# Compressed keys and values of the paged cache: two sequences per matmul, half of the head dimension per gathered buffer

## The chip, the cores and the metric

The kernel runs on one core of one Trainium2 chip. The metric is the device time of one execution in microseconds, as the median of several runs. Names used below: TensorE (PE; its weight loads are PEld), VectorE (DVE), ScalarE (ACT), GpSimd (POOL) and SyncE (SP, which only issues transfers).

## What is computed

One inference step of a decoder layer, for a prompt group (1 sequence of 512 tokens) and a sample group (8 sequences of 4 new tokens, each with 2048 past tokens in a paged cache). Three token mixers run in parallel (causal pooling, sparse attention, a diagonal state space), each gated, merged and projected. The part that matters here is the compressed branch of the sparse attention: blocks of 64 past tokens are each folded into one key and one value per head.

```
past = cache_kv[l][page_table].reshape(bd, past_len, N_KV_ROWS, N_KV_HEADS, HEAD_DIM)
blk = full.reshape(b, nb, BLOCK, N_KV_ROWS, N_KV_HEADS, HEAD_DIM)
kc = jnp.einsum('bnlkd,lde->bnke', blk[:, :, :, 0] + pe_cmp[0][:, None, :], w_phi[0])
vc = jnp.einsum('bnlkd,lde->bnke', blk[:, :, :, 1] + pe_cmp[1][:, None, :], w_phi[1])
```

There are 8 sequences, 16 pages of 128 tokens each, 4 key/value heads of dimension 64, blocks of 64 tokens, so two blocks to a page and 32 to a sequence. The sum over a block's 64 tokens and 64 channels is a contraction of length 4096 per head.

## The kernel before, in words

A dense stream of weight tiles runs through the whole kernel, in an order written out by hand. One unit is a weight block of 128 × 1024; `step` (line 167) issues, in this order: the transfers put off by the step before (`run_deferred`), one slice of each background generator in `bg`, the evacuations due, `w_split` and `w_load` (lines 126 to 146) for later units, and the unit's dense matmuls (`mm3`, lines 148 to 151, three for each product, because float32 is split into a high and a low part). A weight load is issued by SP and waits there until one of three raw buffers is free; a unit's weights are loaded three units ahead and split by ScalarE and VectorE two units ahead. Each engine, and SP's and POOL's queues too, works its instructions off in the order in which the program issues them.

The background generator `main_bg` (line 1623) begins at the seventh step (u = 6) with `g_compress` (line 604), which handles the cache; the state space, the compressed prompt keys, the attention of the prompt and of the samples follow in the same generator.

`g_compress` loads the compression weights `wphi` and works through 16 jobs: 8 sequences times keys and values (k = 0, 1). A job's tile `ca` is 128 partitions × 16 pages × 256 floats, and there are two such tiles, so that one job is fetched while another is used. The partition holds one of two head halves and the token's place in its block; the 256 floats of a page are 4 (two blocks of the page by two heads, `m`), 2 (`k`, called kv2 in the loop) and 32 (`e`, the channels of one half of the head dimension).

`fetch` (line 614) gathers pages. `gather` (line 583) sends pages with an odd index through SP, which reads the page number into a register (lines 585 and 586) and issues a plain transfer, and pages with an even index through GpSimd as an indirect transfer (line 589) that takes its 128 row numbers from IDX. The tiles of jobs 0 and 1 are free at the start; the gathers of a later job wait until the matmuls of the job two before have left the buffer. The first four steps fetch the first job, four pages each. Then each job takes three steps: in a step, 6, 5 and 5 pages of the next job are issued, then the matmuls of 11, 11 and 10 channels `d`.

For each channel `d` there are two matmuls (kv2 = 0, 1; line 632), each with a weight of 128 × 64 in one half of the array's columns and 64 moving columns, one for each page and `m`, which lie 64 floats apart in the tile:

```
t = tiles[n].rearrange("q g (m k e) -> q (g m) k e", m=4, k=2)
pe.matmul(acc_b[kv2 * 64:(kv2 + 1) * 64, :64], lhsT=wphi[:, k, d, :],
          rhs=t[:, :, kv2, d], start=(d == 0), stop=(d == 31))
```

They accumulate over d = 0 to 31 in the PSUM bank `s` (two buffers). ScalarE copies 128 × 64 into `KC` at the end of a job (line 635). A float32 matmul shows as two records in the profile, so line 632 has 16 × 32 × 2 × 2 = 2048. The same GpSimd gathers fetch keys and values (`gk`, `gv`) for the attention of the samples later. Line 875 (state space, 72 moving columns) and line 1244 (attention of the prompt, 128 moving columns) are float32 matmuls with the same 128 × 64 weight shape, whose moving columns lie next to each other.

Of the kernel before, what the change touches and what calls it, by code (L numbers as in the profile page):

```python
# [10 lines left out]
F32 = mybir.dt.float32  # L11
F32R = mybir.dt.float32r
I32 = mybir.dt.int32
AF = mybir.ActivationFunctionType
# [52 lines left out]
def kernel(ctx, tc, a):  # L67
    nc = tc.nc
    pe, dve, act, pool, sp = nc.tensor, nc.vector, nc.scalar, nc.gpsimd, nc.sync
    ctx.enter_context(tc.manual_schedule())  # L70

    def P(name, bufs=1, **kw):
        return tc.tile_pool(name=name, bufs=bufs, **kw)

    def R(name, bufs=1):
        return tc.tile_pool(name=name, bufs=bufs, side="right")
# [9 lines left out]
    def bank(tag, bufs):  # L86
        return psb.tile([128, 512], F32, name=tag, tag=tag, bufs=bufs)
# [28 lines left out]
    ones = consts.tile([128, 128], F32, name="ones")  # L116
    epsb = consts.tile([128, 1], F32, name="epsb")

    # ---------------------------------------------------------------- dense stream
    raw, whi, wlo = {}, {}, {}  # L120
    lo_eng = [dve]
    early = [False]
# [36 lines left out]
    state = {"u": 0}  # L159
# [37 lines left out]
            fn()  # L197
            mid.pop(0)

    # ---------------------------------------------------------------- start: x, first weights  # L200
    xr_s = ExitStack()
    xr_p = xr_s.enter_context(P("xr"))
    XH, XL, XR = [], [], []
    first = wraw_p.tile([128, 8, 128], F32, name="wr")
# [98 lines left out]
            after.append(lambda hf=hf: rms_spread(hf))  # L303
        xr_s.close()

    # ---------------------------------------------------------------- pools of the first part
    att_s = ExitStack()
    kc_p = att_s.enter_context(P("kc", side="right"))
    KC = kc_p.tile([128, 2, 8, 64], F32, name="kc")
# [3 lines left out]
    KN = kc_p.tile([128, 2, 2, 32], F32, name="kn")  # L313
    GQ = kc_p.tile([128, 4, 48], F32, name="gq")

    # ---------------------------------------------------------------- evacuation of in-projection tiles
    done = set()
    sub = {}

# [256 lines left out]
                later(lambda t=t, i=2 * gi + md: sp.dma_start(ypool[i], t))  # L576
        step(u, mms, evac)

    # ---------------------------------------------------------------- compressed keys and values
    IDX = consts.tile([128, 128], I32, name="idx")  # L580
    PT = consts.tile([1, 128], I32, name="ptrow")

    def gather(dst, table, col):
        if col % 2:
            r = sp.value_load(PT[0:1, col:col + 1], min_val=0, max_val=NPOOL - 1)
            sp.dma_start(dst, a[table].rearrange("(g p) x -> g p x", p=128)[bass.ds(r, 1)]
                         .rearrange("g p x -> (g p) x"))
        else:
            pool.indirect_dma_start(out=dst, out_offset=None, in_=a[table],  # L589
                                    in_offset=bass.IndirectOffsetOnAxis(ap=IDX[:, col:col + 1], axis=0))  # L590

    def make_idx():
        pi = consts.tile([128, 1], I32, name="pidx")
        pool.iota(pi, pattern=[[0, 1]], base=0, channel_multiplier=1)
        pf = consts.tile([128, 1], F32, name="pidxf")
        dve.tensor_copy(pf, pi)
        sp.dma_start(PT, a["pt"])
        sp.dma_start(IDX, a["pt"].to_broadcast([128, 128]))
        f = consts.tile([128, 128], F32, name="idxf", bufs=1)
        dve.tensor_copy(f, IDX)  # L600
        dve.tensor_scalar(f, f, 128.0, pf, op0=OP.mult, op1=OP.add)
        dve.tensor_copy(IDX, f)

    def g_compress():
        with ExitStack() as s:
            cp = s.enter_context(R("cmp"))
            wphi = cp.tile([128, 2, 32, 64], F32, name="wphi")
            sp.dma_start(wphi, a["wphi"])
            ca_s = ExitStack()
            cap = ca_s.enter_context(R("ca", 2))  # L610
            jobs = [(b, k) for b in range(8) for k in range(2)]
            tiles = {}

            def fetch(n, pages):
                if n >= len(jobs):
                    return
                b, k = jobs[n]
                if n not in tiles:
                    tiles[n] = cap.tile([128, 16, 256], F32, name="ca")
                for pg in pages:  # L620
                    gather(tiles[n][:, pg, :], f"c{k}", b * 16 + pg)
            for pg in range(0, 16, 4):
                fetch(0, range(pg, pg + 4))
                yield
            for n, (b, k) in enumerate(jobs):
                t = tiles[n].rearrange("q g (m k e) -> q (g m) k e", m=4, k=2)
                acc_b = bank("s", 2)
                for d0, d1, pgs in ((0, 11, (0, 6)), (11, 22, (6, 11)), (22, 32, (11, 16))):
                    fetch(n + 1, range(*pgs))
                    for d in range(d0, d1):  # L630
                        for kv2 in range(2):
                            pe.matmul(acc_b[kv2 * 64:(kv2 + 1) * 64, :64], lhsT=wphi[:, k, d, :],  # L632
                                      rhs=t[:, :, kv2, d], start=(d == 0), stop=(d == 31))
                    yield
                act.activation(KC[:, k, b, :], acc_b[:, :64], AF.Copy)
            yield
            ca_s.close()
        done.add("cache")
# [35 lines left out]
                dve.tensor_scalar(KCP[:, k, :16], KCP[:, k, :16], KCP[:, k, 16:17], None, op0=OP.add)  # L674
                dve.tensor_scalar(KC[:, k], KC[:, k], KCP[:, k, 16:17], None, op0=OP.add)

    # ---------------------------------------------------------------- state space
    SSM = {}
    par_s = ExitStack()

# [343 lines left out]
        par_s.close()  # L1024
        done.add("ssm")

    # ---------------------------------------------------------------- attention of the prompt
    def g_prompt():
        while not all(("q", i) in done for i in range(8)):
            yield  # L1030
# [251 lines left out]
        s.close()  # L1282
        done.add("prompt")

    # ---------------------------------------------------------------- attention of the samples
    def g_decode():
        s = ExitStack()
        dp = s.enter_context(R("dec", 2))
# [253 lines left out]
        s.close()  # L1542
        done.add("decode")

    # ---------------------------------------------------------------- operands of the branches
    YH, YL = {}, {}
    yps = {}

# [59 lines left out]
                yz[k] = (y, z)  # L1608
            yield

    # ---------------------------------------------------------------- run the first part
    make_idx()

    def g_copy():
# [8 lines left out]
    def main_bg():  # L1623
        yield from g_compress()
        early[0] = True
        yield from g_ssm()
        early[0] = False
        yield from g_compress_prompt()
        yield from g_prompt()
        yield from g_decode()  # L1630
        early[0] = True
        att_s.close()
        open_y()
        yield from prep_y(0, ypool, "pz")
        yield from prep_z()
# [38 lines left out]
            fn()  # L1674
    xs.close()

    # ---------------------------------------------------------------- branches
    acc_p = ctx.enter_context(P("accp", 17))
    lg_p = ctx.enter_context(P("lgp", 3))
    xo_p = ctx.enter_context(P("xo", 24))  # L1680
# [134 lines left out]
    for u in range(first_tail, len(UNITS)):  # L1815
# [9 lines left out]
        else:  # L1825
# [4 lines left out]
            m, half = un[1:] if un[1] < 14 else ((14, 0), (15, 0), (14, 1), (15, 1))[u - len(UNITS) + 4]  # L1830
# [7 lines left out]
    normalize(1, range(16))  # L1838


# ------------------------------------------------------------------------------ host side
def col_lists():
    off = np.cumsum([0, 1024, 1024, 1024, 1536, 48, 1024, 1024, 1024, 6144])
    pu, pz, q, kv, ag, az, su, sz, mg = off[:9]
    hd = []
    for p in range(2):
        for g in range(4):
            hd.append(np.concatenate([((2 * p + k) * 4 + g) * 64 + np.arange(64) for k in range(2)]))
    ssm = []
    for i in range(8):  # L1850
        c, g = np.meshgrid(np.arange(2 * i, 2 * i + 2), np.arange(64), indexing="ij")
        ssm.append((g * 16 + c).reshape(-1))
    agc = []
    for j in range(3):
        for p in range(2):
            for g in range(4):
                for k in range(2):
                    agc.append(((2 * p + k) * 4 + g) * 3 + j)
    r = np.arange(128)
    return dict(hd=hd, ssm=ssm, cols={  # L1860
        "pu": [pu + 128 * i + r for i in range(8)], "pz": [pz + 128 * i + r for i in range(8)],
        "q": [q + h for h in hd], "az": [az + h for h in hd],
        "kv": [kv + 128 * i + r for i in range(12)],
        "ag": [ag + np.array(agc + [agc[0]] * 80)],
        "su": [su + s for s in ssm], "sz": [sz + s for s in ssm],
        "mg": [mg + 128 * i + r for i in range(48)]})
# [138 lines left out]
```

## Time and profile before

| | |
|---|---|
| time, median of 3 runs | 2476.44 us (2473.95 to 2479.65) |
| profiled execution, first to last instruction | 2475.4 us |
| TensorE busy | 2345.3 us, 95% |
| VectorE, ScalarE, GpSimd busy | 1111.0, 652.3, 419.9 us |
| line 632 (compression of the cache), matmul busy | 141.5 us in 2048 records, from 84.2 to 573.6 us of the span |
| GpSimd's gathers into `ca` | 128, 126.8 us |
| moved by DMA | 358.32 MB, mean 145 GB/s |

How to read it: the profile is of one execution, and only its span is shown, without what lies around it; the span is 1.0 us under the median. Times of records on TensorE overlap, as matmuls are pipelined: the pace of a burst is its length less one record, over the number of records less one. Some records are missing from the trace, so counts in a stretch are a few per cent low. [...]

### The profile page before, as it was taken

To read this page: it belongs to the slowest core of one execution; us is meant where nothing else is said; L and a number is where in the kernel's file an instruction comes from. 1 tells how busy PE (TensorE), PEld (TensorE's weight loads), DVE (VectorE), ACT (ScalarE), POOL (GpSimd) and SP (SyncE) were. 2 spreads that over 40 slices of the span, in tenths; PEclk is the share of its full clock that TensorE was granted. 3 is DMA by queue.
4 is the path that set the end of the run, shared out by engine and by line. 5 is a ranking of instruction groups with operands and counts; after the bars stand their busy time and mean duration, and the time that the engine had idled before them with its cause. 6 is when DMAs were issued, how large, how long until landed. Compare 5 with 4: busy or idle time off the path is not lost.

```text
span 2475.4 us, 49565 instructions
## 1 busy us (share of the span) xinstructions
PE 2345.3 (95%) x20454; PEld 2236.5 (90%) x20454; DVE 1111.0 (45%) x2157; ACT 652.3 (26%) x1117; POOL 419.9 (17%) x387
## 2 busy tenths in 40 slices
PE   8888888999978999999999999889999999999995
PEld 7888888899978999999999898779999999999995
DVE  6223334114498324676666333322452545554225
ACT  5101111112311111444544222222342222222331
POOL 3122222213235200000000214551000001200003
PEclk9898989999999999999999999999999999999998
DMA  7554564546323666533333357775553555443332
GB/s 241 153 128 125 136 165 124 149 120 137 106 80 108 143 195 195 168 91 96 100 92 87 121 156 246 239 220 170 189 136 118 170 194 191 145 131 111 113 110 91
DMA packets 271650, 358.32 MB, mean 145 GB/s; under 512 B 136129, under 2 KB 186050, under 8 KB 271042
## 3 DMA queue, kind: packets, MB, share of 16 engines
q1 hardware_dynamic: 259138, 321.60, 44.0%
q0 software_dynamic: 12288, 33.57, 4.9%
q8 instruction: 161, 2.64, 0.4%
q14 instruction: 63, 0.52, 0.1%
HBM read 309.26 MB, written 54.13 MB: 147 GB/s over the span
## 4 chain that ended last, share of the span: by engine, by line
PE 89%; DVE 5%; issue 4%; DMA 1%; SPq 0%; ACT 0%; POOL 0%; DVEq 0%; POOLq 0%; ACTq 0%
PE d L149 25%; PE d L151 23%; PE d L150 23%; PE s L632 5%; PE o L1244 2%; PE s L1180 2%; PE t L1220 2%; PE o L1514 1%; DVE t L902 1%; DVE sh L905 1%; PE s L1431 1%; DVE t L904 1%; PE s L963 1%; DVE t L903 1%; PE s L974 1%
## 5 line engine op out<-in xcount | busy, mean ns | idle before, releaser
L149 PE MATMUL d<-xh,whi 128*128 128x272 f32 x3424 | 1022.2, 299 | 24.4 <-DVE e L324 13.4
L151 PE MATMUL d<-xl,whi 128*128 128x272 f32 x3424 | 998.3, 292 | 9.0 <-issue 8.7
L150 PE MATMUL d<-xh,wlo 128*128 128x272 f32 x3424 | 998.1, 291 | 4.5 <-issue 4.0
L149 PEld LDWEIGHTS d<-xh,whi 128*128 128x128 f32 x3424 | 659.7, 193 | 55.7 <-issue 33.2
L151 PEld LDWEIGHTS d<-xl,whi 128*128 128x128 f32 x3424 | 658.9, 192 | 9.1 <-issue 8.0
L150 PEld LDWEIGHTS d<-xh,wlo 128*128 128x128 f32 x3424 | 659.9, 193 | 5.7 <-issue 5.0
L145 DVE TENSOR_TENSOR wlo<-wr,whi 128x1024 fp32r<-128x1024 f32 x298 | 376.8, 1265 | 302.6 <-ACT whi L144 292.9
L144 ACT ACTIVATE whi<-wr 128x1024 fp32r<-128x1024 f32 x309 | 323.0, 1051 | 534.2 <-PE d L151 425.5
L324 DVE TENSOR_TENSOR e<-d,rstd 128x272 f32<-128x272 f32 x186 | 81.6, 439 | 502.5 <-PE d L151 369.6
L589 POOL DMA_INDIRECT ca<-c,idx x128 | 126.8, 990 | 362.3 <-PE s L632 277.9
L632 PE MATMUL s<-ca,wphi 128*64 128x64 f32 x2048 | 141.5, 290 | 46.3 <-issue 39.3
L632 PEld LDWEIGHTS s<-ca,wphi 128*64 128x64 f32 x2048 | 118.6, 158 | 65.6 <-issue 61.1
L589 POOL DMA_INDIRECT gk<-ck,idx x64 | 65.6, 1024 | 622.0 <-ACT e L426 557.0
L151 PE MATMUL d<-ml,whi 128*128 128x272 f32 x512 | 148.1, 289 | 0.0
L149 PE MATMUL d<-yhA,whi 128*128 128x272 f32 x512 | 147.9, 289 | 0.0
L150 PE MATMUL d<-mh,wlo 128*128 128x272 f32 x512 | 147.7, 288 | 0.0
L149 PE MATMUL d<-mh,whi 128*128 128x272 f32 x512 | 147.7, 288 | 0.0
L151 PE MATMUL d<-ylA,whi 128*128 128x272 f32 x512 | 147.6, 288 | 0.0
L150 PE MATMUL d<-yhA,wlo 128*128 128x272 f32 x512 | 147.3, 288 | 0.0
L151 PE MATMUL d<-ylB,whi 128*128 128x272 f32 (+2 forms) x384 | 110.8, 288 | 0.0
L149 PE MATMUL d<-yhB,whi 128*128 128x272 f32 (+2 forms) x384 | 110.7, 288 | 0.0
L150 PE MATMUL d<-yhB,wlo 128*128 128x272 f32 (+2 forms) x384 | 110.5, 288 | 0.0
(391 smaller groups left out, 2861.7 us busy)
## 6 DMA issues: line engine op xcount, KB each, us to landing
wr<-wd SPq DMA_DIRECT2D x309, 512.0 KB
ca<-c SPq DMA_DIRECT2D x128, 128.0 KB
gates<-e SPq DMA_DIRECT2D x48, 272.0 KB
lg<-gates SPq DMA_DIRECT2D x48, 272.0 KB
gk<-ck SPq DMA_DIRECT2D x64, 128.0 KB
gv<-cv SPq DMA_DIRECT2D x64, 128.0 KB
xo<-xT SPq DMA_DIRECT2D x32, 136.0 KB
yT<-yo SPq DMA_DIRECT2D x32, 136.0 KB
```

Source lines behind the costliest of these rows:

```text
L144: act.activation(hi, r, AF.Copy)
L145: lo_eng[0].tensor_tensor(lo, r, hi.bitcast(F32), op=OP.subtract)
L149: pe.matmul(ps, lhsT=h, rhs=xh, start=start, stop=False)
L150: pe.matmul(ps, lhsT=l, rhs=xh, start=False, stop=False)
L151: pe.matmul(ps, lhsT=h, rhs=xl, start=False, stop=stop)
L324: dve.tensor_tensor(out[:, cols(hf)], ps[:, :HALF], rstd[:, cols(hf)], op=OP.mult)
L589: pool.indirect_dma_start(out=dst, out_offset=None, in_=a[table], in_offset=bass.IndirectOffsetOnAxis(ap=IDX[:, col:col + 1], axis=0))
L632: pe.matmul(acc_b[kv2 * 64:(kv2 + 1) * 64, :64], lhsT=wphi[:, k, d, :], rhs=t[:, :, kv2, d], start=(d == 0), stop=(d == 31))
L902: m(t1_, A8[:, 0], prev, op=OP.mult)
L1180: pe.matmul(st[n][k][:, off:off + nk], lhsT=QS[pg][k][:, qt * 128:(qt + 1) * 128], rhs=KS[br, k][j][:, :nk], start=(j == 0), stop=(j == 1))
L1220: pe.transpose(b[:, c:c + 128], st[n][k][:, c:c + 128], ident)
L1244: pe.matmul(o[hs[k], qt * 128:(qt + 1) * 128], lhsT=VN[:, kb, br, pg // 4, hs[k]], rhs=st[n][k][:, off + kb * 128:off + (kb + 1) * 128], s ...
```

## The change

A job is now a pair of sequences, k, and one half h of the 32 channels: 4 × 2 × 2 = 16 jobs. Its tile has the same size, 128 × 32 pages × 128 floats. The host lays the cache out anew, as two tables for each k, with rows of 128 floats (512 bytes) in place of one table with rows of 256: within a row the order is k, e (16 channels), m (4), so that the four columns of a page and channel lie next to each other. Each job needs 32 gathers of 128 rows × 512 bytes where it needed 16 of 128 rows × 1024 bytes; half of them go through GpSimd and half through SP as before. The first four steps fetch 8 pages each, a job's three steps 11, 11 and 10. A matmul has 128 moving columns, 32 runs of four floats with 512 bytes from one run to the next; a job has 16 channels, in steps of 5, 5 and 6, and the accumulation runs over two jobs (h = 0 and 1) before ScalarE copies 128 × 128 into `KC`. Comment lines removed elsewhere in the file are left out here.

```diff
-            jobs = [(b, k) for b in range(8) for k in range(2)]
+            jobs = [(bp, k, h) for bp in range(4) for k in range(2) for h in range(2)]
             tiles = {}
 
             def fetch(n, pages):
                 if n >= len(jobs):
                     return
-                b, k = jobs[n]
+                bp, k, h = jobs[n]
                 if n not in tiles:
-                    tiles[n] = cap.tile([128, 16, 256], F32, name="ca")
+                    tiles[n] = cap.tile([128, 32, 128], F32, name="ca")
                 for pg in pages:
-                    gather(tiles[n][:, pg, :], f"c{k}", b * 16 + pg)
-            for pg in range(0, 16, 4):
-                fetch(0, range(pg, pg + 4))
+                    gather(tiles[n][:, pg, :], f"c{k}{h}", bp * 32 + pg)
+            for pg in range(0, 32, 8):
+                fetch(0, range(pg, pg + 8))
                 yield
-            for n, (b, k) in enumerate(jobs):
-                t = tiles[n].rearrange("q g (m k e) -> q (g m) k e", m=4, k=2)
-                acc_b = bank("s", 2)
-                for d0, d1, pgs in ((0, 11, (0, 6)), (11, 22, (6, 11)), (22, 32, (11, 16))):
+            acc_b = None
+            for n, (bp, k, h) in enumerate(jobs):
+                t = tiles.pop(n).rearrange("q g (k e m) -> q g k e m", m=4, k=2)
+                if h == 0:
+                    acc_b = bank("s", 2)
+                for d0, d1, pgs in ((0, 5, (0, 11)), (5, 10, (11, 22)), (10, 16, (22, 32))):
                     fetch(n + 1, range(*pgs))
                     for d in range(d0, d1):
+                        dd = h * 16 + d
                         for kv2 in range(2):
-                            pe.matmul(acc_b[kv2 * 64:(kv2 + 1) * 64, :64], lhsT=wphi[:, k, d, :],
-                                      rhs=t[:, :, kv2, d], start=(d == 0), stop=(d == 31))
+                            pe.matmul(acc_b[kv2 * 64:(kv2 + 1) * 64, :128], lhsT=wphi[:, k, dd, :],
+                                      rhs=t[:, :, kv2, d, :], start=(dd == 0), stop=(dd == 31))
                     yield
-                act.activation(KC[:, k, b, :], acc_b[:, :64], AF.Copy)
+                if h:
+                    act.activation(KC[:, k, 2 * bp:2 * bp + 2, :].rearrange("q b n -> q (b n)"),
+                                   acc_b[:, :128], AF.Copy)
...
-        v = ck[:, :, k].reshape(npool, 2, 64, 4, 2, 32)
-        ins[f"c{k}"] = C(v.transpose(0, 4, 2, 1, 3, 5)).reshape(npool * 128, 256)
+        v = ck[:, :, k].reshape(npool, 2, 64, 2, 2, 2, 2, 16).transpose(6, 0, 5, 2, 4, 7, 1, 3)
+        for h in range(2):
+            ins[f"c{k}{h}"] = C(v[h]).reshape(npool * 128, 128)
```

## Rows read from the trace of the kernel before

**Rows 1.** The page: busy time by engine, granted clock, and the chain that ended last.

```profile
PE 2345.3 (95%) x20454; PEld 2236.5 (90%) x20454; DVE 1111.0 (45%) x2157; ACT 652.3 (26%) x1117; POOL 419.9 (17%) x387
...
PE 89%; DVE 5%; issue 4%; DMA 1%; SPq 0%; ACT 0%; POOL 0%; DVEq 0%; POOLq 0%; ACTq 0%
PE d L149 25%; PE d L151 23%; PE d L150 23%; PE s L632 5%; PE o L1244 2%; PE s L1180 2%; PE t L1220 2%; PE o L1514 1%; DVE t L902 1%; DVE sh L905 1%; PE s L1431 1%; DVE t L904 1%; PE s L963 1%; DVE t L903 1%; PE s L974 1%
```

**Rows 2.** Lines 632, 875, 1244: count, ns shortest/median/longest, first and last start.

```profile
L632 PE MATMUL s<-ca,wphi x2048: 267/288/368, 84.2 to 573.6; 128*64 128x64 f32 x187
...
L875 PE MATMUL s<-x,m x256: 226/226/277, 598.9 to 658.1; 128*64 128x72 f32 x128
...
L1244 PE MATMUL o<-ptT,vn x640: 272/273/324, 1034.2 to 1399.2; 128*64 128x128 f32 x160
```

**Rows 3.** TensorE in order of time, one burst of each line: start us, length us.

```profile
221.12 2.65 PE L632 MATMUL s<-ca,wphi 128*64 128x64 f32 x44
...
598.92 1.22 PE L875 MATMUL s<-x,m 128*64 128x72 f32 x32
...
1208.16 1.09 PE L1244 MATMUL o<-ptT,vn 128*64 128x128 f32 x16
```

**Rows 4.** One job in order of time, POOL and TensorE: [idle before, releaser].

```profile
232.67 0.95 POOL L589 DMA_INDIRECT ca<-c,idx  x1 [21.35 <-PE s L632]
233.92 0.96 POOL L589 DMA_INDIRECT ca<-c,idx  x1 [0.30 <-issue]
...
238.49 1.09 PE L632 MATMUL s<-ca,wphi 128*64 128x64 f32 x14
239.85 0.27 PE L632 MATMUL s<-ca,wphi 128*64 128x64 f32 x1 [0.27 <-issue]
240.57 0.27 PE L632 MATMUL s<-ca,wphi 128*64 128x64 f32 x1 [0.45 <-issue]
...
241.49 0.95 POOL L589 DMA_INDIRECT ca<-c,idx  x1 [0.30 <-issue]
...
244.13 1.54 PE L632 MATMUL s<-ca,wphi 128*64 128x64 f32 x23 [0.42 <-issue]
...
261.19 0.95 POOL L589 DMA_INDIRECT ca<-c,idx  x1 [18.75 <-DMA pe_s<-poolT]
```

**Rows 5.** Busy time by stretch of GpSimd bursts; the last has none.

```profile
core 0: us, PE busy (x) PEld busy (x) DVE busy (x) ACT busy (x) POOL busy (x), PEclk, DMA share, GB/s
104.45:111.12 6.67, 6.67 (x62) 6.52 (x62) 0.00 (x0) 0.94 (x1) 5.14 (x6) 1.00 0.85 219
111.12:115.90 4.78, 1.74 (x12) 0.83 (x9) 0.00 (x0) 0.00 (x0) 2.52 (x3) 0.86 0.56 165
232.67:239.29 6.62, 6.62 (x61) 6.47 (x61) 0.00 (x0) 0.00 (x0) 5.10 (x6) 1.00 0.75 159
239.29:244.13 4.84, 2.09 (x12) 0.69 (x8) 0.00 (x0) 0.00 (x0) 2.54 (x3) 1.00 0.80 263
...
1539.80:1546.50 6.70, 6.70 (x65) 6.49 (x67) 3.43 (x4) 2.39 (x3) 3.81 (x4) 1.00 1.02 380
1400.35:1412.47 12.12, 12.12 (x101) 12.11 (x99) 2.80 (x3) 1.66 (x3) 9.53 (x9) 1.00 0.69 205
1412.47:1423.40 10.93, 5.40 (x24) 3.87 (x22) 0.00 (x0) 0.00 (x0) 6.69 (x7) 0.77 0.58 185
43.95:57.64 13.69, 13.66 (x107) 13.15 (x105) 4.49 (x13) 3.02 (x5) 10.64 (x11) 1.00 0.81 292
57.64:67.52 9.88, 2.46 (x12) 1.66 (x10) 2.18 (x4) 0.00 (x0) 6.26 (x6) 0.79 0.94 238
441.80:448.50 6.70, 6.70 (x62) 6.38 (x56) 0.00 (x0) 0.00 (x0) 0.00 (x0) 1.00 0.65 179
```

**Rows 6.** The page's costliest groups: GpSimd's gathers into `ca`.

```profile
L589 POOL DMA_INDIRECT ca<-c,idx x128 | 126.8, 990 | 362.3 <-PE s L632 277.9
```

**Rows 7.** SP: three gathers in order of time; its waits, 80 to 580 us.

```profile
256.24 3.75 SPq L586 DMA_DIRECT2D ca<-c  x3
...
SPq L133 <- DVE wlo L145: 144.0, 28, 12.8
SPq L133 <- DVE pe_p L463: 52.0, 5, 13.4
```

## The prediction

> **What bounds the kernel now.** I read the page first, then the compression's matmuls by line, then its bursts in order of time, then busy time by stretch. TensorE is busy for 95% of the span, and the chain that ended last lies 89% on it [rows 1]. So a change counts where it alters what TensorE does or what holds it up; VectorE (45%), ScalarE (26%) and GpSimd (17%) have room. The compression's line 632 alone holds 5% of that chain [rows 1].
>
> Two things in the compression stage matter. The first is the rate of its matmuls. They are float32, so each is two records. One record with 64 columns, read 256 bytes apart, lasts 288 ns; line 875, same weight shape, 72 columns read without a gap, lasts 226 ns; line 1244, 128 columns without a gap, 273 ns [rows 2]. In unbroken bursts (span less one record, over the records less one) the pace is (2.65 − 0.288)/43 = 54.9 ns for line 632, (1.22 − 0.226)/31 = 32.1 ns for line 875, and (1.09 − 0.273)/15 = 54.5 ns for line 1244 [rows 2, 3]. So the gapped read costs about twice what the gapless one does: 128 gapless columns pass in the time of 64 gapped ones.
>
> The second is a hold-up. GpSimd issues its eight gathers of a job in one burst, a gather each 1.26 us. TensorE goes on for some 120 recorded instructions after the first (62 + 62, 61 + 61), then almost stops: 12 matmuls in 4.78 us, 12 in 4.84 us [rows 5]. The matmuls then start 0.7 us apart and wait for nothing the profile shows; full pace returns 2.64 us after the last gather began [rows 4]. Four gathers in a row do not do it (65 matmuls in 6.70 us) [rows 5]. Two bursts of 16 do it for longer: 10.93 us, and 9.88 us at the start of the kernel [rows 5]. There are 128 such gathers [rows 6]: 16 in the first burst and 14 bursts of 8.
>
> **The change, part by part.** *Removed and replaced matmuls.* 16 jobs × 32 × 2 matmuls × 2 records = 2048 records become 16 × 16 × 2 × 2 = 1024, with 128 columns. Before: 2048 × 54.9 ns = 112.4 us. After: the rows hold no read of four floats in a run and then a jump. The bounds are the gapless pace of line 1244, 54.5 ns, and twice that, 109 ns, if every jump hurts as before. I take 54.5, since three of four reads are gapless: 1024 × 54.5 = 55.8 us, so **−56.6 us**, all on TensorE's path. The high bound is 1024 × 109 = 111.6 us, no gain. [...]
>
> *Doubled gathers.* Each job needs 32 gathers of 64 KB where it needed 16 of 128 KB: 16 on GpSimd, 16 on SP. No row shows a gather of 64 KB. Nearest is the 128 KB one at 0.99 us busy [rows 6], 1.26 us from start to start [rows 4]; it has 128 rows as the new one does, so I take 1.26. A burst is then 16 gathers, and the burst still fits a job: GpSimd now idles 18.75 us before the next burst [rows 4], and eight more gathers take 10.1 us. What it costs is TensorE's hold-up. For a burst of 16 I take the mean of the two in the trace, 10.4 us, against 4.8 for eight: 5.6 × 14 = **+78.4 us**. The first burst becomes 32 long (both buffers are free at the start); I double what 16 cost: 20.8 − 9.9 = **+10.9 us**. Bounds: if the hold-up begins after 6.7 us whatever the length, and ends 2.6 us after the sixteenth gather began (15 × 1.26 + 2.6 = 21.5), it is 14.8 us, so 14 × 10 = +140, and for the first burst (31 × 1.26 + 2.6 − 13.7 = 28) +18: together +158. Downwards, if a gather of half the bytes disturbs half as long, 0; and if it drops to the harmless level of the short burst, all is gained: −14 × 4.8 − 9.9 = −77. [...]
>
> *SP's queue.* Three of SP's gathers take 3.75 us, 1.25 each, so eight more are 10 us per job. They stand ahead of each step's weight load. SP waits for freed weight buffers 144.0 + 52.0 = 196 us in this stage of 16 jobs [rows 7], 12 us per job, and weights are loaded three units ahead. So nothing is added, but with little to spare: without that cover each microsecond lands on TensorE, at most 10 × 15 = 150 us, and the conversion of the weights on ScalarE and VectorE would be late next.
>
> *Other edits.* The bytes are the same; DMA engines were 0.56 to 0.85 busy in the compression's bursts [rows 5], so rows of half the length find room. ScalarE evicts 8 times 128 columns instead of 16 times 64, beside 26% load [rows 1]: nothing. Each matmul waits for 32 pages instead of 16; the last land before the next job, by the idle time just named. The weights' order, the steps and everything after the compression stay: nothing.
>
> **Sum.** −56.6 + 78.4 + 10.9 = +32.7 us. On the profiled span of 2475.4 us that is 2508.1. The median of the timed runs, 2476.4, lies 1.0 us above that span, so 2509 us.
>
> **Rivals.** *1. The hold-up follows the bytes (faster).* Place: TensorE in the burst. If half-size gathers disturb half as long, the bursts cost what they did and −56.6 stays: 2420 us; if they become harmless, 2476 − 57 − 77 = 2342. For it: no row has a small gather, and the core moved 263 GB/s in one hold-up against 159 just ahead of it [rows 5]. Against it: the hold-up ends with GpSimd's issuing, and SP's gathers of the same bytes pass with TensorE at full pace (62 matmuls in 6.70 us) [rows 5]. It decides from the point at which a burst of 16 costs less than 4.8 + (56.6 − 10.9)/14 = 8.1 us.
> *2. The new read pattern stays at half rate.* Then the gain of 56.6 is gone: 2566 us. Against it: the pace of the rows without gaps.
> *3. SP becomes late.* If half of the extra 10 us per job lands on TensorE: +75, 2584 us. For it: 12 us of waiting per job against 10 needed.
> *4. The change moves nothing:* a burst of 16 costs about 8.1 us, 2476 us.
>
> **How the numbers follow.** My forecast, a hold-up of 9 to 15 us per burst, has chance 0.55; its own range is 2487 to 2577 (the high end is −56.6 + 158 = +101). Rival 1 has 0.31 (0.26 near 2420, 0.05 lower), rival 2 0.05, rival 3 0.03, rival 4 0.06. The range of 8 in 10 reaches from 2405, a little below rival 1, to 2580: it leaves out the lower part of rival 1, rival 3 and the tails. A measurement of this kernel can tell about 0.2%, 5 us, from no change. Faster by more: rival 1 and a sliver of the forecast's low edge, 0.33. Within 0.2%: rival 4 and its neighbours, 0.08. Slower: 0.59.
>
> **What would show it.** Right: line 632 has 1024 records at about 54.5 ns in bursts, near 273 ns each; GpSimd has 256 gathers into ca at 1.26 us; after each burst's first gather TensorE runs some 120 to 200 instructions, then stalls for 9 to 15 us; jobs take longer than before although they hold 64 records fewer. Wrong: a gather of 0.5 to 0.6 us on GpSimd, or stalls still near 5 us (rival 1); about 340 to 390 ns per record and a pace of 109 ns (rival 2); the hold-up gone and TensorE waiting for weights that DMA brings late (rival 3).

## The result, and the profile after

The changed kernel takes **2597.57 us** (median of 4 runs, 2594.57 to 2599.76) where the kernel before takes 2478.05 on the same chip: the ratio is **1.0489, 95% interval [1.0471, 1.0508]**, 119.5 us slower. The forecast was 2509 us in a range of 2405 to 2580. The sign was right; the size was not, and the range missed it. The right sign is luck in part: experiment 1 shows the same two kernels in a session where the change gains.

One thing has to be said ahead of all else. The study's runs were made in sessions: some kernels and the kernel before, one after the other, on one chip. The median of the kernel before is 2476 to 2478 us in three sessions (the one with the result and two others) and 2350 to 2354 in the other six; each ratio below is taken to the kernel before of its own session. In the first kind TensorE is held up behind GpSimd's bursts, as in [rows 4, 5]: from 40 to 600 us the kernel before has 47.3 us of waits of TensorE's matmuls without a releaser. In the second the same bursts hold nothing up: the profile of the kernel before has no such wait there. I call them held-up and clear sessions. It is not the chip alone: on one chip a session was held-up (2477.1 us) and a later one clear (2352.8).

The page of the changed kernel, held-up session: busy time by engine, the granted clock in 40 slices (in tenths of full speed), the chain by engine, and two of the costliest groups (busy us, mean ns of one | idle before, what ended most of it).

```profile
PE 2326.4 (90%) x19430; PEld 2205.9 (85%) x19430; DVE 1111.0 (43%) x2157; ACT 651.2 (25%) x1109; POOL 541.8 (21%) x515
...
PEclk9778888777999999999999999989999999999998
...
PE 72%; DVE 4%; issue 4%; SPq 1%; DMA 1%; POOL 0%; ACT 0%; DVEq 0%; POOLq 0%
...
L589 POOL DMA_INDIRECT ca<-c,idx x256 | 251.8, 983 | 353.7 <-PE s L635 232.5
...
L635 PE MATMUL s<-ca,wphi 128*64 128x128 f32 x1024 | 89.7, 300 | 85.9 <-issue 54.9
```

Against [rows 1, 6]: TensorE is busy for 90% in place of 95%, although it does 1024 records fewer; the other engines do what they did. GpSimd has 256 gathers of half the bytes, and one costs it 983 ns where the whole one cost 990. The loss lies in slices 2 to 10, the compression.

The changed kernel in order of time: a burst of its matmuls, the first two gathers of a GpSimd burst, and TensorE some 7 us later (start us, length us, engine, line; idle before and releaser in brackets):

```profile
124.59 1.53 PE L635 MATMUL s<-ca,wphi 128*64 128x128 f32 x24
...
126.40 0.95 POOL L589 DMA_INDIRECT ca<-c,idx  x1 [39.53 <-DMA ca<-c]
...
127.66 0.95 POOL L589 DMA_INDIRECT ca<-c,idx  x1 [0.30 <-issue]
...
133.54 0.38 PE L635 MATMUL s<-ca,wphi 128*64 128x128 f32 x2 [0.44 <-issue]
...
138.53 0.37 PE L635 MATMUL s<-ca,wphi 128*64 128x128 f32 x1 [1.75 <-issue]
...
146.27 0.39 PE L150 MATMUL d<-xh,wlo 128*128 128x272 f32 x1 [1.72 <-issue]
```

And busy time by stretch: ahead of a hold-up, in it, and behind it, then the first burst (columns as in [rows 5]).

```profile
126.40:132.83 6.43, 6.43 (x58) 6.28 (x57) 0.02 (x1) 0.00 (x0) 4.91 (x6) 1.00 0.71 188
132.83:149.10 16.27, 4.14 (x17) 2.27 (x15) 0.00 (x0) 0.00 (x0) 10.37 (x11) 0.63 0.24 69
149.10:166.37 17.27, 17.26 (x139) 16.63 (x140) 5.20 (x7) 2.36 (x3) 0.00 (x0) 0.86 0.45 116
...
58.01:91.75 33.74, 6.62 (x18) 4.67 (x19) 2.17 (x4) 0.00 (x0) 21.95 (x23) 0.56 0.38 98
```

The 24 matmuls at 124.59 have a pace of (1.53 − 0.273)/23 = 54.7 ns: the matmul term is as forecast. Gathers start 1.26 us apart, as before. TensorE goes on for 6.43 us after the first, then makes 17 matmuls in **16.27 us**, where eight gathers cost 4.78 us. No dependency is named (issue), the DMA engines are 0.24 busy, and the granted clock, 1.00 ahead of it, averages 0.63 in it (0.50 from 138 us on). The first burst, of 32, holds TensorE up for **33.74 us**.

Its waits of TensorE and of SP's queue, 40 to 760 us (in total, times, longest us):

```profile
PE s L635 <- issue: 54.9, 53, 5.5
PE d L151 <- issue: 35.3, 26, 2.4
PE d L149 <- issue: 32.9, 32, 2.4
PE d L150 <- issue: 32.0, 29, 2.6
PE s L635 <- DMA ca<-c: 20.1, 2, 18.8
PE s L635 <- DMA ca<-c,idx: 10.9, 4, 5.0
...
SPq L133 <- DVE wlo L145: 70.6, 18, 8.0
```

New beside the hold-ups are 31 us in which TensorE waits for pages (`ca`); for the kernel before the profile names no wait for pages there, though it puts 6.8 us of its line 632 down to other transfers. SP's spare time (its waits for weight buffers) has shrunk from the 144.0 us of [rows 7] to 70.6, although this window is the longer.

### The profile page after: what moved, and what is told of

Read it like the earlier page. It is cut to its first block, busy times and chain, and to the rows that moved or that the text cites. A ratio compares the mean times of both kernels' runs of the same rounds, so it can differ in the third digit from the quotient of the medians.

```text
span 2592.8 us, 48395 instructions
## 1 busy us (share of the span) xinstructions
PE 2326.4 (90%) x19430; PEld 2205.9 (85%) x19430; DVE 1111.0 (43%) x2157; ACT 651.2 (25%) x1109; POOL 541.8 (21%) x515
## 4 chain that ended last, share of the span: by engine, by line
PE 72%; DVE 4%; issue 4%; SPq 1%; DMA 1%; POOL 0%; ACT 0%; DVEq 0%; POOLq 0%
PE d L149 21%; PE d L151 20%; PE d L150 20%; PE o L1249 2%; PE s L1185 2%; PE t L1225 2%; PE s L635 1%; PE o L1519 1%; DVE t L907 1%; PE s L1436 1%; DVE sh L910 1%; DVE t L909 1%; PE s L968 1%; DVE t L908 1%; PE s L979 1%
## 5 line engine op out<-in xcount | busy, mean ns | idle before, releaser
L151 PE MATMUL d<-xl,whi 128*128 128x272 f32 x3424 | 1007.0, 294 | 40.4 <-issue 40.1
L149 PEld LDWEIGHTS d<-xh,whi 128*128 128x128 f32 x3424 | 667.1, 195 | 102.5 <-issue 79.1
L151 PEld LDWEIGHTS d<-xl,whi 128*128 128x128 f32 x3424 | 666.2, 195 | 45.2 <-issue 44.3
L150 PEld LDWEIGHTS d<-xh,wlo 128*128 128x128 f32 x3424 | 667.4, 195 | 38.2 <-issue 38.1
L589 POOL DMA_INDIRECT ca<-c,idx x256 | 251.8, 983 | 353.7 <-PE s L635 232.5
L635 PE MATMUL s<-ca,wphi 128*64 128x128 f32 x1024 | 89.7, 300 | 85.9 <-issue 54.9
L635 PEld LDWEIGHTS s<-ca,wphi 128*64 128x64 f32 x1024 | 66.8, 149 | 98.5 <-issue 94.8
L1721 POOL TENSOR_TENSOR acc<-acc,lg 128x544 f32<-128x544 f32 x16 | 21.8, 1361 | 444.0 <-DVE lg L1717 444.0
```

Of the source, the lines that this page charges most:

```text
L149: pe.matmul(ps, lhsT=h, rhs=xh, start=start, stop=False)
L150: pe.matmul(ps, lhsT=l, rhs=xh, start=False, stop=False)
L151: pe.matmul(ps, lhsT=h, rhs=xl, start=False, stop=stop)
L635: pe.matmul(acc_b[kv2 * 64:(kv2 + 1) * 64, :128], lhsT=wphi[:, k, dd, :], rhs=t[:, :, kv2, d, :], start=(dd == 0), stop=(dd == 31))
```

## Experiments

| kernel | clear: us, ratio to the kernel before | held-up: us, ratio |
|---|---|---|
| kernel before, medians of the sessions | 2350 to 2354 | 2476 to 2478 |
| changed kernel | 2345.4, 0.9965 [0.9954, 0.9975] | 2597.6, 1.0489 [1.0471, 1.0508] |
| GpSimd's gathers split | 2353.3, 0.9995 [0.9985, 1.0005]; 2349.1, 0.9995 [0.9985, 1.0006] | 2650.1, 1.0702 [1.0678, 1.0727] |
| changed, 20 of 32 pages on GpSimd | – | 2670.2, 1.0780 [1.0753, 1.0806] |
| new order alone | 2317.2, 0.9842 [0.9826, 0.9859]; 2310.3, 0.9825 [0.9809, 0.9842] | 2445.9, 0.9873 [0.9854, 0.9893] |
| SP's loads split | – | 2487.4, 1.0045 [1.0029, 1.0060] |
| all pages on SP | 2365.8, 1.0046 [1.0030, 1.0063] | – |
| changed, all pages on SP | 2613.9, 1.1107 [1.1089, 1.1126] | – |
| new order, all pages on SP | 2343.7, 0.9957 [0.9941, 0.9974]; 2342.1, 0.9951 [0.9934, 0.9968] | – |
| pauses | 2351.8, 0.9990 [0.9981, 1.0000]; 2352.3, 0.9997 [0.9987, 1.0006] | – |
| new order, pauses | 2315.8, 0.9847 [0.9831, 0.9864]; 2316.0, 0.9838 [0.9821, 0.9854] | – |

Theory A, after the result: GpSimd's gathers hold TensorE up by their number in a row, and the change doubles that number. The first four kernels (order alone, all pages on SP, split, pauses) fell on a clear session, where the kernel before took 2354.4 us. So three of them could not tell theory A from its rivals, and the next question was what the two kernels do there unchanged.

**1. Both kernels unchanged, clear session.**

> The kernel before unchanged, for a trace of it beside the experiments: the experiments so far showed no hold-up of TensorE at GpSimd's gathers at all, and a kernel before of 2354 us where it had been 2478. Theory F (hold-up belongs to the place or state of the machine that a program runs in, not to the kernel): no gaps behind bursts of 8, clock 0.988, 2354 us. Theory A (it belongs to the bursts): gaps of 4 to 5 us in 13 of 15 bursts, 2478 us.

> The changed kernel unchanged, beside the kernel before. Theory F (the whole loss came from hold-ups of instruction supply that this place does not have): the matmul term (-56.6 us) remains, SyncE's lateness takes back up to 30, so 2354 - 57 + (0 to 30) = 2300 to 2330 us, faster by 1 to 2.3%. Theory G (the loss lies in the change's transfers and page waits): 2400 us or more, slower.

The kernel before took 2355.6 us. The changed kernel took 2345.4, ratio 0.9965 [0.9954, 0.9975] to the kernel before of that session (2354.2): 9 us less, a small gain but clear of the interval, where the held-up session has it 119.5 slower. Theory F holds in its sign; the gain is below its 24 to 54 us. A burst of 16 of the changed kernel there, by stretch (its first 7 us, the next 15.5, and the rest with the whole next burst), and TensorE's waits, 40 to 600 us:

```profile
100.20:107.20 7.00, 7.00 (x68) 6.75 (x66) 1.09 (x3) 0.00 (x0) 5.48 (x6) 1.00 0.74 192
107.20:122.70 15.50, 15.50 (x147) 14.80 (x144) 4.19 (x6) 2.38 (x3) 9.81 (x12) 1.00 0.64 169
122.70:145.40 22.70, 22.47 (x210) 21.48 (x209) 4.52 (x9) 2.14 (x3) 15.26 (x16) 1.00 0.62 163
```

```profile
PE s L635 <- DMA ca<-c,idx: 25.0, 6, 6.9
PE s L635 <- DMA ca<-c: 21.2, 5, 7.9
```

TensorE runs 147 matmuls where it ran 17, at the full clock. By the waits that the profile names, what takes back the larger part of the 56.6 us there is the pages' lateness: 46 us of waits for `ca`, 11 in the kernel before. If nothing else differs between the two kinds of session, which is not shown, they also price the hold-ups as a whole, with the clock behind them (0.50 for 5 us after the one at 111.12 us of the kernel before): 2478 − 2354 = 124 us in the kernel before, 2598 − 2345 = 252 in the changed one. Their difference, 128 us, less the 9 us gained, is the measured loss.

**2. Number or bytes: GpSimd's gathers split.** Each of GpSimd's gathers in the kernel before becomes two of half a row, into the same place; bytes, matmuls and SP's loads stay.

```diff
+    def gather_halves(dst, table, col):
+        for h in range(2):
+            pool.indirect_dma_start(out=dst[:, h * 128:(h + 1) * 128], out_offset=None, in_=a[f"{table}{h}"],
+                                    in_offset=bass.IndirectOffsetOnAxis(ap=IDX[:, col:col + 1], axis=0))
...
-                    gather(tiles[n][:, pg, :], f"c{k}", b * 16 + pg)
+                    if pg % 2:
+                        gather(tiles[n][:, pg, :], f"c{k}", b * 16 + pg)
+                    else:
+                        gather_halves(tiles[n][:, pg, :], f"c{k}", b * 16 + pg)
```

> The kernel before with each GpSimd gather of a compression page cut into two of half a row (512 bytes per partition): the same bytes into the same tile, the same matmuls, twice as many GpSimd gathers. Theory A (by the number in a row): hold-ups of about 16 us per burst of 16 as in the changed kernel and about 33 us for the first of 32, the clock as low as there, total 2478 + 14 x 11 + 24 = about 2655 us (2600 to 2700). Rival D (by the bytes or the time that the transfers take): hold-ups stay at 4 to 6 us, total 2478 us within 20.

> The same kernel as e5_split (each GpSimd gather of a page cut into two of half a row), for a chip on which the kernel before takes 2478. Theory A (number of gathers in a row): hold-ups of about 16 us behind each burst of 16, 33 us behind the first of 32, total 2478 + 14 x 11 + 23 = about 2655 us (2600 to 2700). Rival D (bytes): 4 to 6 us, 2478 us. On a chip where the kernel before takes 2354 it tells nothing new.

> The kernel before with each GpSimd gather of a page cut into two of half a row, same bytes and matmuls. On a chip where the kernel before takes 2478, theory A (number of gathers in a row): hold-ups of about 16 us behind each burst of 16 and 33 us behind the first of 32, total 2478 + 14 x 11 + 23 = about 2655 us (2600 to 2700). Rival D (bytes, or the order, width or half rows of the change): 4 to 6 us, 2478 us within 10. On a chip where the kernel before takes 2350: no difference again.

In two clear sessions it made no difference (0.9995 both times). In the held-up one it took **2650.1 us** (two executions, 2649 and 2651) against 2475.6, as theory A had worked out. Its stretches ahead of a hold-up and in it:

```profile
127.06:134.21 7.15, 6.97 (x65) 6.56 (x63) 0.00 (x0) 0.93 (x1) 5.63 (x6) 1.00 0.70 176
134.21:149.80 15.59, 3.77 (x19) 2.13 (x18) 1.68 (x2) 0.00 (x0) 9.68 (x11) 0.55 0.26 66
```

19 matmuls in 15.59 us, as in the changed kernel, with the matmuls, the order and the bytes of the kernel before. So the number of gathers makes the hold-up longer; neither their bytes nor the wider matmul does. Rival D falls. Since GpSimd's gathers start 1.26 us apart at 1024 bytes a row as at 512, these runs cannot tell the number from the time that GpSimd spends on gathers in a row.

**3. A third length.** The changed kernel with bursts of 20.

```diff
-    def gather(dst, table, col):
-        if col % 2:
+    def gather(dst, table, col, on_sp=None):
+        if (col % 2) if on_sp is None else on_sp:
...
-                    gather(tiles[n][:, pg, :], f"c{k}{h}", bp * 32 + pg)
+                    gather(tiles[n][:, pg, :], f"c{k}{h}", bp * 32 + pg, pg % 8 in (1, 4, 6))
```

> The changed kernel with 20 of a job's 32 pages on GpSimd and 12 on SyncE (16 and 16 before). Where nothing holds TensorE up: SyncE is relieved of 5 us a job, waits for ca fall from 46 us to under 20, total 2345 - 25 = about 2320 us, faster than the kernel before by 1 to 2%. Where GpSimd's bursts do (kernel before at 2478): each hold-up is 5 us longer than in the changed kernel, 2598 + 14 x 5 and more, 2650 to 2700 us.

2670.2 us, in the range given for a held-up session. A hold-up of it:

```profile
142.07:163.05 20.98, 4.88 (x15) 3.34 (x15) 1.67 (x2) 0.00 (x0) 13.78 (x14) 0.62 0.27 84
```

4.78 us for 8 gathers, 16.27 for 16, 20.98 for 20: 1.2 to 1.4 us for each gather more, close to the 1.26 us at which GpSimd issues them.

**4. The order alone.** The kernel before with the new order in a row; 64 columns, whole pages, 16 per job.

```diff
-                t = tiles[n].rearrange("q g (m k e) -> q (g m) k e", m=4, k=2)
+                t = tiles[n].rearrange("q g (k e m) -> q g k e m", m=4, k=2)
...
-                                      rhs=t[:, :, kv2, d], start=(d == 0), stop=(d == 31))
+                                      rhs=t[:, :, kv2, d, :], start=(d == 0), stop=(d == 31))
...
-        v = ck[:, :, k].reshape(npool, 2, 64, 4, 2, 32)
-        ins[f"c{k}"] = C(v.transpose(0, 4, 2, 1, 3, 5)).reshape(npool * 128, 256)
+        v = ck[:, :, k].reshape(npool, 2, 64, 2, 2, 2, 32)
+        ins[f"c{k}"] = C(v.transpose(0, 5, 2, 4, 6, 1, 3)).reshape(npool * 128, 256)
```

> The kernel before with only the new order inside a page's row (the four key positions of a page side by side), still 64 columns per matmul, 16 pages of 128 KB per job, 8 of them by GpSimd. Theory A (TensorE is held up by the number of gathers that GpSimd issues in a row, so the change lost its time by doubling that number, not by its order or its width): the 2048 matmuls issue every 29 to 32 ns instead of 54.9, hold-ups stay at 4 to 5 us for a burst of 8 gathers, total 2478 - 50 = about 2428 us (2410 to 2445). Rival B (the new order is what costs, by its read pattern or its packets): hold-ups of 10 us or more or a pace no better than 54.9 ns, and a total at or over 2478 us.

> The same kernel as e1_order (new order in the row alone, 16 whole pages a job), for a chip on which the kernel before takes 2478. Theory A: hold-ups stay at 4 to 5 us, the matmul term of 50 us is gained in full or nearly: 2425 to 2445 us. Rival B (order or pace of the matmuls lengthens the hold-ups, since a faster TensorE drains what it has been given sooner): each of 15 hold-ups starts 1 us sooner at most, so 2440 to 2460 us. On a chip where the kernel before takes 2354 it repeats 2317.

> The new order in the row alone, 64 columns, 16 whole pages a job. On a chip where the kernel before takes 2478, theory A: hold-ups stay at 4 to 5 us, the matmul term is gained nearly in full: 2425 to 2445 us. Rival B (a faster TensorE drains its instructions sooner or the order disturbs the transfers): 2450 us or more. On a chip where the kernel before takes 2350: 2312 again.

It is faster in both kinds of session: 0.9842 and 0.9825 in clear ones, 0.9873 in the held-up one (2445.9 us, 30 us gained: between the two forecasts of that run's expectation, 2425 to 2445 for theory A and 2450 or more for rival B, and inside the 2440 to 2460 that the second expectation gave rival B). A burst of its matmuls in a clear session, then a hold-up in the held-up one:

```profile
91.85 1.39 PE L632 MATMUL s<-ca,wphi 128*64 128x64 f32 x40
```

```profile
101.68:108.18 6.50, 6.50 (x67) 6.34 (x66) 0.16 (x1) 0.94 (x1) 4.97 (x6) 1.00 0.83 211
108.18:113.16 4.98, 1.63 (x13) 0.68 (x7) 0.00 (x0) 0.00 (x0) 2.73 (x3) 0.84 0.60 174
```

A record of it lasts 222 ns, so the pace is (1.39 − 0.222)/39 = **29.9 ns** for 64 columns, against 54.7 for 128 in the changed kernel. The 2048 records then need 61.2 us, 51.2 less than before. So the order brings 51.2 of the 56.6 us; the width brings 5.4, and it is for the width that the pages were halved and the gathers doubled. The hold-ups stay at about 5 us, the one shown at 4.98: the longer ones of rival B in the first expectation are not there. Of the 51.2 us some 30 reach the held-up total and 37 to 40 the clear one. The rest is not accounted for.

**5. What SP's queue costs.** Four kernels move or double SP's loads. In the first, each page that SP loads in the kernel before is cut into two loads of half a row, as in experiment 2 for GpSimd. In the others SP takes all pages of a job: 16 whole ones (order as before, and new), or the changed kernel's 32.

```diff
-                    gather(tiles[n][:, pg, :], f"c{k}", b * 16 + pg)
+                    gather(tiles[n][:, pg, :], f"c{k}", b * 16 + pg, True)
```

> The kernel before with each page that SyncE loads cut into two loads of half a row; GpSimd's 8 gathers a job stay whole; same bytes, same matmuls, 64 columns. SyncE issues 16 loads a job in place of 8, 10 us a job more. Theory H (SyncE's extra issues take back most of the matmul term where nothing holds TensorE up, as the trace of the changed kernel has it: 46 us of waits for ca against 11): TensorE's waits for ca grow to 20 to 50 us and the total is 15 to 45 us over the kernel before beside it. Rival I (SyncE's waits for weight buffers, 150 us, cover the 10 us a job): within 5 us of the kernel before. If the kernel before stands at 2478 here (hold-ups present), they stay 4 to 5 us per burst of 8, since SyncE's loads don't make them.

Held-up session: 1.0045 [1.0029, 1.0060], 10 us slower, with 10.5 us of waits for `ca`. That lies between theory H (15 to 45) and rival I (within 5). TensorE's waits without a releaser at these matmuls, 40 to 760 us, are 40.4 us in sum, where the kernel before has 39.3. Doubling SP's loads did not lengthen TensorE's hold-ups as doubling GpSimd's gathers does (155.2 us of such waits in experiment 2).

> The kernel before with all 16 page gathers of a compression job issued by SyncE as plain transfers, none by GpSimd. Theory A: the hold-ups of the compression stretch (14 of some 4.8 us, one of 9.9, 77 us together) are gone, and the time at half clock behind each goes with them, so 2478 - 77 = 2401 us, down to 2360 with the clock. Rival C (what the changed kernel lost is SyncE's lateness: it has 20 us of page loads per job here as it has in the changed kernel): weight blocks come late, waits of TensorE for xhi/whi or ca grow by 20 us or more, and the time stays within 30 us of 2478 or above it.

> The kernel before with the new order in a row (64 columns, 16 pages a job) and all compression gathers on SyncE. Where gathers by GpSimd hold nothing up: 2317 us (order alone) + 12 (SyncE alone cost that) = about 2329 us. Where they do (kernel before at 2478): 2478 - 50 - 77 and the clock = 2300 to 2360 us.

> The new order, 64 columns, 16 whole pages a job, all of them on SyncE. On a chip where the kernel before takes 2478, theory A: no hold-up in the compression, so 2344 (its time on a chip without hold-ups) plus some 40 us for the bursts of the attention of the samples, 2360 to 2395 us, faster than the order alone (2446). Rival C (SyncE's lateness takes its place): 2430 us or more. On a chip where the kernel before takes 2350: 2344 again.

> The changed kernel with all 32 page gathers of a job on SyncE, none on GpSimd. SyncE then needs 32 x 1.25 = 40 us per job at about 36 us of matmuls: where GpSimd's gathers hold nothing up, slower than the changed kernel by 20 us or more (16 jobs x 1 to 4 us, and weight loads that come late); where they do (kernel before at 2478, changed kernel at 2598), faster than the changed kernel by 100 us or more.

All four runs were in clear sessions, so they could not show hold-ups going. They do show SP's limit. With 16 whole pages on SP the total is 11 us longer than before (1.0046). The new order, all on SP, gains 0.43 and 0.49%, less than the order alone; about 2329 us had been expected of it there, and it took 2343.7. With 32 pages the changed kernel takes 2613.9 us, and TensorE waits for what SP brings:

```profile
PE s L635 <- DMA ca<-c: 275.1, 16, 20.3
```

**6. Pauses.** The kernel before with six memsets of a scratch tile on GpSimd, 4.8 us, after every fourth of its gathers; then the same with the new order.

```diff
+            gap = cp.tile([128, 768], F32, name="gap")
...
                     gather(tiles[n][:, pg, :], f"c{k}", b * 16 + pg)
+                    if pg % 8 == 6:
+                        for _ in range(6):
+                            pool.memset(gap, 0.0)
```

> The kernel before with some 4.5 us of GpSimd memsets of a scratch tile after every fourth of its compression gathers; nothing else moves. Theory A (a run of gathers without a pause is what holds TensorE up, and a pause lets it refill): bursts of 4 hold nothing up, as in the one burst of 4 in the trace of before, total 2478 less some 50 to 100 us, 2380 to 2430 us. Rival E (each gather costs TensorE its share of instructions wherever it lies, or any GpSimd activity does): the hold-ups are only spread or grow by the pause, total 2470 us or more.

> The kernel before with some 4.5 us of GpSimd memsets of a scratch tile after every fourth of its compression gathers, nothing else moved. On a chip where the kernel before takes 2478, theory A (an unbroken run of gathers; a pause refills): bursts of 4 hold nothing up, the 77 us of hold-ups and the clock behind them go, 2380 to 2410 us, near the 2352 of the chips without hold-ups plus what the attention of the samples keeps. Rival E (each gather takes its share wherever it lies): 2470 us or more. On a chip where the kernel before takes 2350: no difference again.

> The new order in the row (64 columns, 16 whole pages a job) with six memsets of a scratch tile on GpSimd, 4.8 us, after every fourth of its compression gathers. On a chip where the kernel before takes 2478 and the order alone 2446, theory A (the unbroken run counts, a pause refills): no hold-up over 1 us in the compression, 2317 (order alone without hold-ups) plus some 40 us for the attention of the samples, 2345 to 2385 us. Rival E (each gather for itself): hold-ups as long in sum as before, 2435 us or more. On a chip where the kernel before takes 2350: 2312 to 2320, as the order alone.

> The new order in the row (64 columns, 16 whole pages a job) with 4.8 us of GpSimd memsets after every fourth of its compression gathers. On a chip where the kernel before takes 2478 and the order alone 2446, theory A (the unbroken run counts, a pause refills): no hold-up over 1 us in the compression, 2345 to 2385 us. Rival E (each gather for itself): hold-ups as long in sum as before, 2435 us or more. On a chip where the kernel before takes 2350: 2316 again.

All four met clear sessions. There the pauses cost nothing (0.9990 and 0.9997; with the order 0.9847 and 0.9838, as the order alone). Whether they remove the hold-ups where those occur is open.

## Why the prediction was wrong

*Matmuls, −56.6 us: right.* 1024 records at 54.7 ns (54.5 forecast, from line 1244). Runs of four floats, 16 bytes, go at the gapless pace here; in experiment 4 the same runs take 29.9 ns for 64 columns in place of 54.9. Rival 2, half rate, falls.

*Gathers, 1.26 us each at half the bytes too: right.* 983 ns busy and 1.26 us from start to start at 64 KB, where [rows 4, 6] have 990 ns and 1.26 us at 128 KB. Rival 1, by bytes, falls with it and with experiment 2.

*Hold-ups, +78.4 and +10.9 us: this step failed, on size.* That GpSimd's doubled gathers lengthen them was right. I took 10.4 us for a burst of 16 and 20.8 for the first of 32. From the first gap over 0.5 us to the last, the changed kernel's 14 have a mean of 15.4 us and the first has 33.0; by the same count the kernel before has 4.5 and 9.9. By this count they grow in sum from some 72 to 248 us, by 176 where 89 was forecast; less the matmuls that run inside them (about 8 and 25 us at full pace), TensorE loses some 158 us more.

The mean of the two bursts of 16 in [rows 5] was the wrong row to take. Both have gathers that start further apart. The gathers of the shorter one at its start, and of the other in its middle, in the trace of the kernel before:

```profile
43.95 1.13 POOL L589 DMA_INDIRECT ca<-c,idx  x1 [7.79 <-DVE sdiag L292]
45.39 1.86 POOL L589 DMA_INDIRECT ca<-c,idx  x1 [0.30 <-issue]
47.55 0.96 POOL L589 DMA_INDIRECT ca<-c,idx  x1 [0.31 <-issue]
...
1406.74 1.80 POOL L589 DMA_INDIRECT gk<-ck,idx  x1 [0.30 <-issue]
1408.86 0.96 POOL L589 DMA_INDIRECT gk<-ck,idx  x1 [0.31 <-issue]
```

Starts 2.1 us apart stand there, and the hold-up began 12 to 14 us after the first gather in place of 6.6 to 6.7. That the wider spacing puts the start off is read from such bursts side by side; no experiment changed it alone. The changed kernel has such a burst too, with three starts 1.5 to 1.6 us apart; its hold-up begins 11.17 us in and lasts 12.19:

```profile
206.44:217.61 11.17, 11.17 (x101) 10.85 (x99) 4.19 (x8) 2.65 (x4) 8.73 (x9) 1.00 0.53 107
217.61:229.80 12.19, 3.98 (x14) 2.47 (x12) 0.00 (x0) 0.00 (x0) 7.62 (x8) 0.69 0.49 133
```

A burst of eight at an even pace carried the right model: the onset stays at some 6.5 us, each further gather adds its own 1.26. My upper bound, 14.8 us a burst and 28 for the first, was that model. It gave +101 us in all, 2577; I put it at the end of the range, not in the sum. The bound itself was short as well: full pace returns 3.8 us after the last of 16 gathers began, and 2.6 after the last of eight.

The row by which [rows 5] had four gathers as harmless proved less than I took from it: its 6.70 us end about where a hold-up begins after eight. The trace goes on at full pace, so that reading stands (the row for SP's gathers holds three of them; experiment 5 says more):

```profile
1546.50:1551.00 4.50, 4.50 (x69) 3.86 (x60) 3.06 (x6) 2.44 (x5) 2.85 (x3) 1.00 0.85 264
```

*SP, nothing: wrong, by a smaller amount.* SP's waits were no full cover. Doubling its loads alone costs 10 us in the held-up session (experiment 5), and in a clear one TensorE of the changed kernel waits 46 us for pages. Rival 3 was given 0.03, and a part of it is real. The 31 us of the held-up trace are not all of this kind. 18.8 of them are one wait, for which SP needed 13.36 us for five gathers. These five lie in a burst of GpSimd (gathers from 458.18 to 477.97), and SP itself is slowed in such places. Five of its gathers outside a hold-up, five in the hold-up at 132.83, and the five in question; then six at the same place of a burst in the clear session:

```profile
123.48 4.98 SPq L586 DMA_DIRECT2D ca<-c  x5
...
133.57 15.52 SPq L586 DMA_DIRECT2D ca<-c  x5
...
468.23 13.36 SPq L586 DMA_DIRECT2D ca<-c  x5
```

```profile
111.52 6.30 SPq L586 DMA_DIRECT2D ca<-c  x6
```

In neither of the two slow rows does the profile name anything that these gathers waited for. So the hold-up is not TensorE's alone, and some 8 of the 18.8 us (13.36 − 4.98) come from it and not from SP's doubled number.

*The sum.* −56.6 + 158 + 31 = +132 against +119.5 measured. What lies in parallel among these, and how the 31 divide between SP's number and the hold-ups, was not taken apart. *What I left out:* that the hold-ups might not belong to the kernel alone. Nothing in one trace could show it, and in a clear session the forecast of slower would have had the wrong sign.

## What to carry to other kernels

Before doubling the number of gathers to make a matmul wider, see whether the same columns per nanosecond come from the order in memory alone: here the order brought 51 of the 57 us, and by itself it beats both kernels in both kinds of session. Price a stall from the row whose conditions (even spacing, length) are those of the new case, and put a model that explains onset and end of each row into the sum, not into the range. Take a profile of the unchanged kernel in a second session before a stall without a named releaser is charged to the kernel.

## What the runs showed of the hardware

Runs of eight and more GpSimd gathers hold TensorE up in some sessions and not in others, with the same program: 4.8, 16.3 and 21.0 us for 8, 16 and 20 gathers, or nothing. GpSimd's gathers start 1.26 us apart in the changed kernel's held-up session and in a clear one of the kernel with pauses. SP's loads slow down in the same stretches (five in 15.52 us in place of 4.98). What decides it is open; chip and program alone do not.

One thought is that TensorE runs out of instructions. No run shows that it does. The page of the changed kernel has a queue named for them (packets, MB, share of the DMA engines):

```profile
q8 instruction: 154, 2.52, 0.4%
```

That is 16 KB a packet. Which engine's instructions they are, no view says. If all are TensorE's, its 2 × 19430 matmuls and weight loads have 65 bytes each and a packet holds some 250 of them, an estimate from these counts alone. The trace does not bear out that TensorE stops when a packet is used up. From the first gather of an even burst to the hold-up some 60 matmuls run with as many weight loads (58 and 57 from 126.40 us), by that estimate half a packet, and the onset follows the gathers and not the packets. The hold-up at 132.83 begins 6.43 us after the first gather, and a packet starts with it (between 132.80 and 133.00). The next one begins 6.42 us after its first gather (166.37), although the last packet started 9 us ahead of it (between 163 and 164), and none starts until its end:

```profile
172.79:189.11 16.32, 5.31 (x20) 2.77 (x17) 0.00 (x0) 0.00 (x0) 10.38 (x11) 0.66 0.24 64
```

What it is that stops, no run here shows; the instruction supply of theory F and the refilling of theory A are conjectures.

Columns that lie together in runs of 16 bytes take 29.9 ns where a matmul has 64 of them and 54.7 ns where it has 128, 0.47 and 0.43 ns a column; 64 columns that lie 256 bytes apart take 54.9 ns, 0.86 a column.
